# Stick-breaking attention on one core: masks ahead of logits, ScalarE in written order, weight casts three units ahead

## The chip, the cores and the metric

The kernel runs on one core of one Trainium2 chip. The metric is the device time of one execution in microseconds (us); the time of the kernel before is the median of three runs. The profile shows one execution of the same program, taken by the hardware profiler. Engines are called as the profile calls them: PE (TensorE, matmuls), DVE (VectorE), ACT (ScalarE), POOL (GpSimd), SP (SyncE, which issues most DMAs).

## The reference

A trunk of four layers on 256 frames of width 1024 in float32: layers 0 and 3 mix tokens by retention, layer 1 by a Conformer convolution, layer 2 by stick-breaking attention; each is followed by a squared-ReLU MLP. The change touches layer 2 alone:

```
def stick_breaking_mixer(xn, w_in, q_gain, k_gain, w_out):
    proj = xn @ w_in
    q, k, v = jnp.split(proj, 3, axis=-1)
    q = rms_norm(q by head, q_gain); k = rms_norm(k by head, k_gain)     # 16 heads of 64
    ...
    z = einsum('bhqd,bhkd->bhqk', q, k) * scale                           # blocks of 128 queries
    mask = s_idx[None, :] < t_idx[:, None]
    log_1mb = where(mask, log_sigmoid(-z), 0.0)
    log_w = log_sigmoid(z) + cumsum(log_1mb, reverse=True) - log_1mb
    a = where(mask, exp(log_w), 0.0)
    ...
    return (a @ v, heads joined) @ w_out
```

## The kernel before

Nearly all the time is matmuls with streamed weights. A *unit* is a tile of 128x1024 float32 weights. For each unit, SP brings it by DMA (two units to one transfer of 1 MB, into one of three `raw` tiles), ACT casts it to a rounded high part `wh` (`nc.scalar.copy`, L350), DVE subtracts to get the low part `wl` (L357), and PE multiplies with both. `wh` and `wl` have five buffers each. The function `unit` does this; the order of the units is fixed by the list `PLAN`.

In `stick`, the string `SB_ORDER` gives the order of steps, each a letter and its indices: `p b kb` is one weight unit of the projection of q and k for head group b (four heads; `mm_a`, 12 matmuls of 512 columns, L918 to L920); `n b` is the RMS norm of that group (two Squares on ACT, L1372; on DVE two sums L1374, a chain of small operations for the inverse root, and two scalings L1384); `u b` and `t b` transpose q and k on PE (L1394) and copy them out on ACT (L1399, L1406); `l b` makes the logits of the group in three PSUM tiles: z2 (second 128 queries against second 128 keys, L1420) and z0, z1 (first 128 keys against all queries, for the even and the odd heads, L1433); the mask is added by a matmul of an identity with a tile of 0 and -1e30 (L1427). `s b` is the softplus of the three tiles (ACT Abs L1445, Exp L1446, Ln L1447; DVE max-and-add L1448, rounding L1450, remainder L1451); `w b i` adds the reverse cumulative sum to tile i by matmuls with a triangle (L1458; L1462 for the second key block), whose operands are the rounding and the remainder, and takes the Exp on ACT (L1464); `v c kb` is a unit of the projection of v; `m b` multiplies weights and values (L1485, L1488). Logits and transposes share a PSUM pool of four tiles named `mis`: three logits tiles of one group and one more, so that a transpose needs a tile that an Exp of the group before has read. `res_pairs` with `out_proj` is the output projection.

The order of PE's instructions is as written (`manual_schedule` for PE). The other engines' instructions are put in order by the framework's scheduler, from its own estimates. On the chip each engine runs its list in order and waits at semaphores. Buffers of a pool are given out in the order of the program, and a write waits until the last reader of the buffer is done.

```
with self.tc.manual_schedule(engines={mybir.EngineType.PE}):
    go(SB_ORDER[0])
    self.out_proj("sb_w_out", j, G["y"], 2, 4, nxt, before=between)
```

Of the kernel before, what the change touches and what calls it, by code (L numbers as in the profile page):

```python
# [9 lines left out]
F32R = mybir.dt.float32r  # L10
I32 = mybir.dt.int32
AF = mybir.ActivationFunctionType
ALU = mybir.AluOpType
AX = mybir.AxisListType

P = 128
D = 1024
S = 256
# [12 lines left out]
DST = 6  # L31

SB_ORDER = (
    "p00 p01 r p02 p03 p10 n0 p11 p12 p13 u0 t0 p20 n1 l0 s0 p21 p22 w02 p23 n2 w00 u1 t1 p30 l1 p31 p32 s1"
    " w01 w12 p33 w10 u2 t2 w11 v00 n3 l2 s2 v01 v02 w22 v03 u3 t3 w20 v10 l3 v11 s3 w21 v12 w32 v13 w31 w30"
    " m0 m1",
    "m2 m3",
)

# [197 lines left out]
def v3(ap, a, b):  # L239
    return ap.rearrange("p (a b) -> p a b", a=a, b=b)  # L240


class Trunk:
# [342 lines left out]
                    nc.tensor.matmul(o[:, :S], wl[:, kk, cs], z[:, :S], start=False, stop=k == 7, **kw)  # L586
        return [self.sum_w(ps[0]), self.sum_w(ps[1])]

    def res_pairs(self, name, l, acts, nkb, group, evac, before=None):
        for g in range(4 // group):  # L590
            ps = [self.acc() for _ in range(group)]
            for kb in range(nkb):
                if before is not None:
                    before(kb)
                for p in range(group):
                    w = self.unit((name, l, "b", kb, (g * group + p) * 256))
                    self.mm_b(ps[p], w, acts, kb * 4, kb == 0, kb == nkb - 1)
                    if kb == nkb - 1:
                        evac(g * group + p, ps[p])


    def ffn(self, i, nxt):
        nc = self.nc
        last = nxt is None
# [113 lines left out]
    def retention(self, j, nxt):  # L718
# [107 lines left out]
        for h in range(RH):  # L826
# [21 lines left out]
            rs = self.rsqrt(m, 2, "v")  # L848
            G = self.col(2, "G")
            nc.vector.tensor_mul(G, rs, fh)  # L850
            gn = [self.bigt() for _ in range(2)]
# [8 lines left out]
            for t in range(2):  # L860
                sg, u = self.bigt(), self.tmp()
                nc.scalar.activation(out=sg, in_=pg[t], func=AF.Silu, scale=self.r[:, t : t + 1])
                nc.vector.scalar_tensor_tensor(
                    out=u, in0=yb[t], scalar=G[:, t : t + 1], in1=gn[0], op0=ALU.mult, op1=ALU.mult
                )
# [19 lines left out]
    def out_begin(self, nxt, bias=None):  # L885
# [15 lines left out]
            self.norm_pair(p, *nxt)  # L901

        return evac

    def out_proj(self, name, l, y, nkb, group, nxt, bias=None, before=None):
        self.res_pairs(name, l, lambda k: y[k], nkb, group, self.out_begin(nxt, bias), before)


    def mm_a(self, ps, w, kb):
        nc = self.nc  # L910
# [430 lines left out]
    def stick(self, j, nxt):  # L1341
        nc = self.nc
        self.table("natural_log_exp_and_others")
        kw = dict(skip_group_check=True)
        Ur, m1r, idr, negr = (self.cp.tile([P, P], F32R, name=f"{k}r", tag=f"{k}r") for k in ("U", "m1", "id", "neg"))
        for t, key in ((Ur, "U"), (m1r, "m1"), (idr, "id"), (negr, "neg")):
            nc.vector.tensor_copy(t, self.c(key, P))
        G = {}


        def proj(b, kb):
            if kb == 0:
                G["p", b] = self.acc(), self.acc()
            w = self.unit(("sb_w_in", j, "qk", kb, b * 256))
            self.mm_a(G["p", b], w, kb)

        def rnorm():
            self.norm_r(False)

            G["r64"], G["rr"] = self.col(2, "r64"), self.col(4, "rr")  # L1360
            nc.vector.tensor_scalar(out=G["r64"], in0=self.r2, scalar1=1.0 / DH, scalar2=None, op0=ALU.mult)
# [27 lines left out]
        def trans(b, isk=1):  # L1389

            pt = self.mis()
            for pr in range(2):
                for t in range(2):
                    nc.tensor.transpose(  # L1394
                        pt[:, pr * S + t * P : pr * S + (t + 1) * P],
                        G["sc", b, t][:, isk * S + pr * P : isk * S + (pr + 1) * P], self.id,
                    )
            G["qk"[isk], b] = self.bigt()
            nc.scalar.activation(out=G["qk"[isk], b], in_=pt, func=AF.Copy, scale=self.p(("sq", "sk")[isk]))  # L1399
            if not isk:  # L1400

                G["f", b] = f = self.bigt()
                nc.gpsimd.memset(f, 0.0)
                for e in range(2):
                    r = slice(e * DH, (e + 1) * DH)
                    nc.scalar.activation(  # L1406
                        out=v3(f[r, e * S : (e + 1) * S], 2, P), in_=v3(pt, 2, S)[r, :, P:], func=AF.Copy,
                        scale=self.p("sq")[r],
                    )

        def logits(b):


            z2, z0, z1 = self.mis(), self.mis(), self.mis()
            zb = G["z", b] = [z0, z1, z2]
            kT, qT = G["k", b], G["q", b]
            for e in range(2):
                for pr in range(2):
                    o = (2 * e + pr) * P
                    nc.tensor.matmul(  # L1420
                        zb[2][:, o : o + P], kT[:, pr * S + P : (pr + 1) * S], G["f", b][:, o : o + P],
                        start=o == 0, stop=False, **kw,
                    )

            def mask(z):
                n = z.shape[1]
                nc.tensor.matmul(z, idr, negr.unsqueeze(1).to_broadcast([P, n, P]), start=False, stop=True, **kw)  # L1427

            mask(v3(zb[2], 4, P))
            for pr in range(2):  # L1430
                for e in range(2):
                    r = slice(e * DH, (e + 1) * DH)
                    nc.tensor.matmul(  # L1433
                        zb[e][:, pr * S : (pr + 1) * S], kT[r, pr * S : pr * S + P], qT[r, pr * S : (pr + 1) * S],
                        start=pr == 0, stop=False, **kw,
                    )
            for e in range(2):
                mask(v3(zb[e], 2, S)[:, :, :P])

        def soft(b):  # L1440

            zb = G["z", b]
            for i in (2, 0, 1):
                ab, ex, ln, l = self.tmp(), self.tmp(), self.tmp(), self.tmp()
                nc.scalar.activation(out=ab, in_=zb[i], func=AF.Abs)  # L1445
                nc.scalar.activation(out=ex, in_=ab, func=AF.Exp, scale=-1.0)  # L1446
                nc.scalar.activation(out=ln, in_=ex, func=AF.Ln, bias=1.0)  # L1447
                nc.vector.scalar_tensor_tensor(out=l, in0=zb[i], scalar=0.0, in1=ln, op0=ALU.max, op1=ALU.add)  # L1448
                lh, ll = self.bigt(F32R), self.bigt(F32R)
                nc.vector.tensor_copy(lh, l)  # L1450
                nc.vector.tensor_sub(ll, l, lh)  # L1451
                G["l", b, i] = lh, ll

        def weights(b, i):

# [10 lines left out]
        def values(cb, kb):  # L1466
            if kb == 0:
                G["pv", cb] = self.acc(), self.acc()
            pv = G["pv", cb]
            w = self.unit(("sb_w_in", j, "a", kb, 2 * D + cb * 512))  # L1470
            self.mm_a(pv, w, kb)
            if kb == 3:
                for t in range(2):
                    G["v", cb, t] = self.bigt()
                    nc.scalar.activation(out=G["v", cb, t], in_=pv[t], func=AF.Copy, scale=self.r[:, t : t + 1])

        def mix(b):
            A = [G["A", b, i] for i in range(3)]
# [13 lines left out]

        G["y"] = []
        table = {
            "p": proj, "r": rnorm, "n": norm, "u": lambda b: trans(b, 0), "t": trans, "l": logits, "s": soft, "w": weights, "v": values, "m": mix
        }
        def go(steps):
            for step in steps.split():
                table[step[0]](*(int(c) for c in step[1:]))

        def between(kb):
            if kb == 1:
                go(SB_ORDER[1])

        with self.tc.manual_schedule(engines={mybir.EngineType.PE}):
            go(SB_ORDER[0])
            self.out_proj("sb_w_out", j, G["y"], 2, 4, nxt, before=between)

    def run(self):
        self.table("silu_and_others")  # L1510
# [49 lines left out]
```

## Time and profile before

| | |
|---|---|
| time, median of 3 runs (lowest to highest) | 1342.24 us (1342.0 to 1342.4) |
| span of the profiled execution, first to last instruction | 1340.3 us |
| PE busy | 1330.8 us, 99% of the span |
| DVE, ACT, POOL busy | 984.0, 781.3, 134.0 us |
| granted TensorE clock, mean | 0.999 |
| layer 2's attention, from the first projection matmul to the first of the value product | 661.4 to 750.5 us of the span |

The profiled execution is given by its span alone; the median of the timed runs lies 1.9 us above it. A busy PE is read with care: matmuls overlap, and the profile models their ends, so a row's length (0.39 us for 512 columns) is longer than the distance from one start to the next (0.23 us). Where a row of the timeline has "x8", the time is that of eight matmuls together; a float32 matmul shows as two.

### The profile page before, as it was taken

What the parts mean: (1) busy time and instruction counts of PE and PEld (TensorE: products, weight loads), DVE (VectorE), ACT (ScalarE), POOL (GpSimd) and SP (SyncE); (2) the same over time, 40 slices, a digit from 0 to 9 for tenths busy, and PEclk for the clock granted to TensorE, in tenths of its full rate; (3) what the DMA queues carried; (4) which work ended last, traced back from release to release, by engine and by line L of the source; (5) the groups of instructions that cost most, each with busy time, mean ns of one, the idle gap of its engine ahead of it and who ended that gap; (6) DMA issues with size and microseconds to landing.
All of it is one profiled execution on the core that took longest, in us unless ns stands there. A gap on an engine that the chain in (4) does not pass through costs nothing.

```text
span 1340.3 us, 20902 instructions
## 1 busy us (share of the span) xinstructions
PE 1330.8 (99%) x8285; PEld 1170.4 (87%) x8285; DVE 984.0 (73%) x1642; ACT 781.3 (58%) x1205; POOL 134.0 (10%) x123
## 2 busy tenths in 40 slices
PE   9999999999999999999999999999999999999998
PEld 7988888888999998888878898888888888988886
DVE  6977769775688698765687587755697777788643
ACT  7555546664457477744578577744565555555442
POOL 3200002000169210000100010000120000100000
PEclk9999999999999999999999999999999999999999
DMA  7555555555545645555453345555555454555551
GB/s 283 210 184 190 187 181 197 189 188 189 188 159 145 219 170 203 190 192 192 172 183 126 126 166 190 192 190 194 177 181 187 174 188 173 189 189 189 204 188 63
DMA packets 41586, 244.56 MB, mean 182 GB/s; under 512 B 4624, under 2 KB 9104, under 8 KB 14096
## 3 DMA queue, kind: packets, MB, share of 16 engines
q1 hardware_dynamic: 40768, 240.86, 50.7%
q10 hardware_dynamic: 720, 2.36, 0.5%
q8 instruction: 65, 1.06, 0.3%
q14 instruction: 33, 0.27, 0.1%
HBM read 241.27 MB, written 1.93 MB: 181 GB/s over the span
## 4 chain that ended last, share of the span: by engine, by line
PE 99%; DMA 0%; ACT 0%; DVE 0%; issue 0%; SPq 0%
PE acc L524 34%; PE acc L520 18%; PE acc L683 6%; PE acc L918 6%; PE acc L920 6%; PE acc L919 6%; PE acc L504 4%; PE acc L505 4%; PE acc L506 4%; PE acc L1087 1%; PE acc L1220 1%; PE mis L809 1%; PE mis L870 1%; PE mis L400 0%; PE mis L1458 0%; PE acc L585 0%
## 5 line engine op out<-in xcount | busy, mean ns | idle before, releaser
L357 DVE TENSOR_TENSOR wl<-raw,wh 128x1024 fp32r<-128x1024 f32 (+1 forms) x440 | 546.5, 1247 | 242.8 <-ACT wh L350 236.4
L350 ACT CAST wh<-raw 128x1024 fp32r<-128x1024 f32 (+1 forms) x440 | 456.5, 1042 | 353.1 <-PE acc L524 164.8
L524 PE MATMUL acc<-z,wh 128*128 128x512 f32 x1120 | 387.4, 392 | 0.0
L520 PE MATMUL acc<-z,wl 128*128 128x256 f32 x1120 | 310.2, 281 | 0.0
L524 PE MATMUL acc<-big,wh 128*128 128x512 f32 x864 | 298.8, 392 | 0.0
L524 PEld LDWEIGHTS acc<-z,wh 128*128 128x128 f32 x1120 | 208.3, 187 | 44.7
L520 PE MATMUL acc<-big,wl 128*128 128x256 f32 x864 | 238.5, 280 | 0.5 <-DVE t L568 0.5
L520 PEld LDWEIGHTS acc<-z,wl 128*128 128x128 f32 x1120 | 211.1, 189 | 1.7
L524 PEld LDWEIGHTS acc<-big,wh 128*128 128x128 f32 x864 | 161.0, 187 | 34.8
L520 PEld LDWEIGHTS acc<-big,wl 128*128 128x128 f32 x864 | 162.4, 189 | 2.3 <-DVE t L568 1.3
L918 PE MATMUL acc<-wh,z 128*128 128x512 f32 x352 | 138.0, 392 | 0.0
L920 PE MATMUL acc<-wh,z 128*128 128x512 f32 x352 | 137.3, 390 | 0.0
L919 PE MATMUL acc<-wl,z 128*128 128x512 f32 x352 | 137.2, 390 | 0.0
L455 POOL TENSOR_TENSOR t<-t,t 128x512 f32<-128x512 f32 x23 | 36.2, 1573 | 893.7 <-ACT t L450 850.6
L567 ACT COPY t<-acc 128x256 f32<-128x256 f32 x176 | 61.8, 373 | 100.6 <-PE acc L524 99.3
L568 DVE TENSOR_TENSOR t<-acc,t 128x256 f32<-128x256 f32 x176 | 69.1, 421 | 34.9 <-ACT t L567 34.8
L683 PE MATMUL acc<-wh,big 128*128 128x512 f32 x256 | 79.3, 390 | 0.0
L920 PEld LDWEIGHTS acc<-wh,z 128*128 128x128 f32 x352 | 66.1, 188 | 14.7 <-issue 0.8
L918 PEld LDWEIGHTS acc<-wh,z 128*128 128x128 f32 x352 | 66.1, 188 | 14.1 <-issue 0.8
L919 PEld LDWEIGHTS acc<-wl,z 128*128 128x128 f32 x352 | 66.1, 188 | 13.1
L504 PE MATMUL acc<-z,wh 128*128 128x256 f32 x256 | 72.5, 284 | 0.0
L505 PE MATMUL acc<-z,wh 128*128 128x256 f32 x256 | 72.4, 283 | 0.0
(259 smaller groups left out, 1813.0 us busy)
## 6 DMA issues: line engine op xcount, KB each, us to landing
raw<-in_w SPq DMA_DIRECT2D x214, 1024.0 KB, 4.8
raw<-in_w SPq DMA_DIRECT2D x8, 512.0 KB, 8.9
big<-in_gn SPq DMA_DIRECT2D x16, 256.0 KB, 5.2
raw<-hd SPq DMA_DIRECT2D x8, 263.0 KB, 4.8
raw<-hd SPq DMA_DIRECT2D x8, 131.5 KB, 3.6
x<-in_x SPq DMA_DIRECT2D x4, 256.0 KB, 6.3
wh<-in_w ACTq DMA_DIRECT2D x2, 512.0 KB, 6.4
wl<-in_w ACTq DMA_DIRECT2D x2, 512.0 KB, 8.5
```

Of the source, the lines that this page charges most:

```text
L350: nc.scalar.copy(hi[:, s], src[:, s])
L357: self.nc.vector.tensor_sub(lo[:, s], src[:, s], hi[:, s])
L504: nc.tensor.matmul(o, wh[:, kk, cs], ah, start=st, stop=False, **kw)
L505: nc.tensor.matmul(o, wh[:, kk, cs], al, start=False, stop=False, **kw)
L520: mm = nc.tensor.matmul(ps[m][:, :S], wl[:, kk, cs], a[:, :S], start=first and kk == 0, stop=False, **kw)
L524: nc.tensor.matmul(ps[m], wh[:, kk, cs], a, start=False, stop=last and kk == 3, **kw)
L567: nc.scalar.copy(o[:, s], ps[m][:, S:])
L568: nc.vector.tensor_add(o[:, s], ps[m][:, :S], o[:, s])
L683: self.tc.keep_in_program_order(nc.tensor.matmul(ps[t], l, r[:, kk], start=False, stop=kb * 2 + kk == 31 and n == 2, **kw))
L918: nc.tensor.matmul(ps[t], zh[:, s], wh[:, kk], start=k == 0, stop=False, skip_group_check=True)
L919: nc.tensor.matmul(ps[t], zh[:, s], wl[:, kk], start=False, stop=False, skip_group_check=True)
L920: nc.tensor.matmul(ps[t], zl[:, s], wh[:, kk], start=False, stop=k == 7, skip_group_check=True)
```

## The change

Four things change, all in `stick`; the arithmetic stays, up to the order in which the sums of a logits tile are formed.

1. In `logits`, the mask matmuls come first and start the accumulation; before, the mask of each tile came after its logits.
2. ACT joins PE in the written order (`manual_schedule`), so that the scheduler no longer places ACT's instructions in the attention layer and its output projection. For this the softplus is split into one step per tile (`s b i`) and placed between projection units, the copy of v out of PSUM is a step of its own (`c`), and the norms move: `n1` and `n3` to ahead of the projection unit that they stood behind (`p20`, `v00`), `n2` to behind the transposes that it stood ahead of.
3. `weight(n)` calls `unit` for units up to n + 3 (`SB_AHEAD`) when unit n is used, so that ACT's casts stand three units ahead in the written order; before, the scheduler placed them.
4. `res_pairs` and `out_proj` are written out in `stick`, with the same order of matmuls.

```
 SB_ORDER = (
-    "p00 p01 r p02 p03 p10 n0 p11 p12 p13 u0 t0 p20 n1 l0 s0 p21 p22 w02 p23 n2 w00 u1 t1 p30 l1 p31 p32 s1"
-    " w01 w12 p33 w10 u2 t2 w11 v00 n3 l2 s2 v01 v02 w22 v03 u3 t3 w20 v10 l3 v11 s3 w21 v12 w32 v13 w31 w30"
-    " m0 m1",
+    "p00 p01 r p02 p03 p10 n0 p11 p12 p13 u0 t0 n1 p20 l0 s02 p21 s00 p22 s01 w02 p23 w00 u1 t1 n2 p30 l1 s12 p31 s10"
+    " p32 s11 w01 w12 p33 w10 u2 t2 w11 n3 v00 l2 s22 v01 s20 v02 s21 w22 v03 u3 t3 w20 c0 v10 l3 s32 v11 s30 w21 v12 s31"
+    " w32 v13 w31 w30 c1 m0 m1",
     "m2 m3",
 )
+SB_AHEAD = 3
...
+        keys = [("sb_w_in", j, "qk", kb, b * 256) for b in range(4) for kb in range(4)]
+        keys += [("sb_w_in", j, "a", kb, 2 * D + c * 512) for c in range(2) for kb in range(4)]
+        keys += [("sb_w_out", j, "b", kb, p * 256) for kb in range(2) for p in range(4)]
+        ready = {}
+
+        def weight(n):
+            while len(ready) <= min(n + SB_AHEAD, len(keys) - 1):
+                ready[len(ready)] = self.unit(keys[len(ready)])
+            return ready[n]
...
             zb = G["z", b] = [z0, z1, z2]
             kT, qT = G["k", b], G["q", b]
+
+            def mask(z):
+                n = z.shape[1]
+                nc.tensor.matmul(z, idr, negr.unsqueeze(1).to_broadcast([P, n, P]), start=True, stop=False, **kw)
+
+            mask(v3(z2, 4, P))
+            for e in range(2):
+                mask(v3(zb[e], 2, S)[:, :, :P])
...
-            mask(v3(zb[2], 4, P))
...
-            for e in range(2):
-                mask(v3(zb[e], 2, S)[:, :, :P])
...
-        def soft(b):
...
+        def soft(b, i):
...
-        with self.tc.manual_schedule(engines={mybir.EngineType.PE}):
+        with self.tc.manual_schedule(engines={mybir.EngineType.PE, mybir.EngineType.Activation}):
             go(SB_ORDER[0])
-            self.out_proj("sb_w_out", j, G["y"], 2, 4, nxt, before=between)
+            evac = self.out_begin(nxt)
+            ps = [self.acc() for _ in range(4)]
+            for kb in range(2):
+                if kb == 1:
+                    go(SB_ORDER[1])
+                for p in range(4):
+                    self.mm_b(ps[p], weight(24 + 4 * kb + p), lambda k: G["y"][k], kb * 4, kb == 0, kb == 1)
+                    if kb == 1:
+                        evac(p, ps[p])
```

What it moves in the built program, at three places. Names are those of the tiles with their numbers (`mis` the PSUM tiles, `big` and `t2` SBUF tiles, `wh`, `wl`, `raw` the weights), written to the left of the arrow. The line numbers of the changed kernel lie some lines off those of the profile before.

PE, the logits of the first head group, before:

```order
L1420 MATMUL mis_1321_7413<-big_1303_7355,big_1305_7364 128x128 x4
L1427 MATMUL mis_1321_7413<-negr_7150,idr_7149 128x512
L1433 MATMUL mis_1322_7414<-big_1302_7353,big_1305_7364 128x256
L1433 MATMUL mis_1323_7415<-big_1302_7353,big_1305_7364 128x256
L1433 MATMUL mis_1322_7414<-big_1302_7353,big_1305_7364 128x256
L1433 MATMUL mis_1323_7415<-big_1302_7353,big_1305_7364 128x256
L1427 MATMUL mis_1322_7414<-negr_7150,idr_7149 128x2x128
L1427 MATMUL mis_1323_7415<-negr_7150,idr_7149 128x2x128
```

and now:

```order
L1411 MATMUL mis_1328_7427<-negr_7150,idr_7149 128x512
L1411 MATMUL mis_1329_7428<-negr_7150,idr_7149 128x2x128
L1411 MATMUL mis_1330_7429<-negr_7150,idr_7149 128x2x128
L1419 MATMUL mis_1328_7427<-big_1311_7371,big_1313_7380 128x128 x4
L1426 MATMUL mis_1329_7428<-big_1310_7369,big_1313_7380 128x256
L1426 MATMUL mis_1330_7429<-big_1310_7369,big_1313_7380 128x256
L1426 MATMUL mis_1329_7428<-big_1310_7369,big_1313_7380 128x256
L1426 MATMUL mis_1330_7429<-big_1310_7369,big_1313_7380 128x256
```

The three masks moved to the front; the eight matmuls are the same.

ACT, from the Ln of the first group's last tile to the copies of the second group's transposes, before:

```order
L1447 ACTIVATE t2_1338_7453<-t2_1337_7452 128x512
L1372 ACTIVATE t2_1351_7518<-acc_1306_7366 128x512
L1372 ACTIVATE t2_1353_7523<-acc_1307_7367 128x512
L350 CAST wh_1411_7732<-raw_1410_7730 128x1024
L1464 ACTIVATE big_1347_7499<-mis_1321_7413 128x512
L1464 ACTIVATE big_1360_7548<-mis_1322_7414 128x512
L1399 ACTIVATE big_1362_7555<-mis_1361_7550,prm_91 128x512
L1406 ACTIVATE big_1363_7557<-mis_1361_7550,prm_91 64x256 x2
L1399 ACTIVATE big_1365_7566<-mis_1364_7561,prm_91 128x512
```

and now:

```order
L1436 ACTIVATE t2_1350_7501<-t2_1349_7500 128x512
L1453 ACTIVATE big_1354_7513<-mis_1328_7427 128x512
L351 CAST wh_1356_7517<-raw_1355_7515 128x1024
L1453 ACTIVATE big_1358_7537<-mis_1329_7428 128x512
L1390 ACTIVATE big_1360_7544<-mis_1359_7539,prm_91 128x512
L1397 ACTIVATE big_1361_7546<-mis_1359_7539,prm_91 64x256 x2
L1390 ACTIVATE big_1363_7555<-mis_1362_7550,prm_91 128x512
L1363 ACTIVATE t2_1365_7558<-acc_1324_7409 128x512
L1363 ACTIVATE t2_1367_7563<-acc_1325_7410 128x512
```

The two Squares of norm 2 went from ahead of the first Exp to behind the copies, and the cast from ahead of the first Exp to behind it.

DVE, the second group's scalings and the first group's z2 and z0 tiles, before:

```order
L1384 TENSOR_TENSOR t2_1319_7409<-acc_1279_7251,sbf_1318_7407 128x512
L1384 TENSOR_TENSOR t2_1320_7411<-acc_1280_7252,sbf_1318_7407 128x512
L1448 SCALAR_TENSOR_TENSOR t2_1327_7430<-mis_1321_7413,t2_1326_7429 128x512
L1450 CAST big_1328_7435<-t2_1327_7430 128x512
L1451 TENSOR_TENSOR big_1329_7436<-t2_1327_7430,big_1328_7435 128x512
L357 TENSOR_TENSOR wl_1378_7621<-raw_1376_7618,wh_1377_7620 128x1024
L1448 SCALAR_TENSOR_TENSOR t2_1333_7442<-mis_1322_7414,t2_1332_7441 128x512
```

and now:

```order
L1375 TENSOR_TENSOR t2_1322_7405<-acc_1287_7267,sbf_1321_7403 128x512
L1375 TENSOR_TENSOR t2_1323_7407<-acc_1288_7268,sbf_1321_7403 128x512
L1437 SCALAR_TENSOR_TENSOR t2_1334_7444<-mis_1328_7427,t2_1333_7443 128x512
L1439 CAST big_1335_7449<-t2_1334_7444 128x512
L358 TENSOR_TENSOR wl_1339_7456<-raw_1337_7453,wh_1338_7455 128x1024
L1440 TENSOR_TENSOR big_1336_7450<-t2_1334_7444,big_1335_7449 128x512
L1437 SCALAR_TENSOR_TENSOR t2_1343_7474<-mis_1329_7428,t2_1342_7473 128x512
```

A weight subtraction now stands between the rounding and the remainder of a logits tile. Over the twelve logits tiles this is so at seven; before, at two.

More of the change, by code (lines that the diff above doesn't have):

```diff
@@ L587, in pairs_qk @@
         return [self.sum_w(ps[0]), self.sum_w(ps[1])]
[L589 to L599, printed above, removed]
     def ffn(self, i, nxt):
@@ L903, in out_begin @@
         return evac
-    def out_proj(self, name, l, y, nkb, group, nxt, bias=None, before=None):
-        self.res_pairs(name, l, lambda k: y[k], nkb, group, self.out_begin(nxt, bias), before)
     def mm_a(self, ps, w, kb):
@@ L1353, in proj @@
                 G["p", b] = self.acc(), self.acc()
-            w = self.unit(("sb_w_in", j, "qk", kb, b * 256))
-            self.mm_a(G["p", b], w, kb)
+            self.mm_a(G["p", b], weight(4 * b + kb), kb)
         def rnorm():
@@ L1421, in logits @@
                         zb[2][:, o : o + P], kT[:, pr * S + P : (pr + 1) * S], G["f", b][:, o : o + P],
-                        start=o == 0, stop=False, **kw,
+                        start=False, stop=False, **kw,
                     )
-            def mask(z):
-                n = z.shape[1]
-                nc.tensor.matmul(z, idr, negr.unsqueeze(1).to_broadcast([P, n, P]), start=False, stop=True, **kw)
-            mask(v3(zb[2], 4, P))
             for pr in range(2):
@@ L1434, in logits @@
                         zb[e][:, pr * S : (pr + 1) * S], kT[r, pr * S : pr * S + P], qT[r, pr * S : (pr + 1) * S],
-                        start=pr == 0, stop=False, **kw,
+                        start=False, stop=False, **kw,
                     )
-            for e in range(2):
-                mask(v3(zb[e], 2, S)[:, :, :P])
-        def soft(b):
[L1442 to L1452, printed above, removed]
+        def soft(b, i):
+            z = G["z", b][i]
+            ab, ex, ln, l = self.tmp(), self.tmp(), self.tmp(), self.tmp()
+            nc.scalar.activation(out=ab, in_=z, func=AF.Abs)
+            nc.scalar.activation(out=ex, in_=ab, func=AF.Exp, scale=-1.0)
+            nc.scalar.activation(out=ln, in_=ex, func=AF.Ln, bias=1.0)
+            nc.vector.scalar_tensor_tensor(out=l, in0=z, scalar=0.0, in1=ln, op0=ALU.max, op1=ALU.add)
+            lh, ll = self.bigt(F32R), self.bigt(F32R)
+            nc.vector.tensor_copy(lh, l)
+            nc.vector.tensor_sub(ll, l, lh)
+            G["l", b, i] = lh, ll
         def weights(b, i):
@@ L1469, in values, with values_out @@
             pv = G["pv", cb]
[L1470 to L1475, printed above, removed]
+            self.mm_a(pv, weight(16 + 4 * cb + kb), kb)
+        def values_out(cb):
+            for t in range(2):
+                G["v", cb, t] = self.bigt()
+                nc.scalar.activation(
+                    out=G["v", cb, t], in_=G["pv", cb][t], func=AF.Copy, scale=self.r[:, t : t + 1]
+                )
         def mix(b):
@@ L1494, in stick @@
         table = {
-            "p": proj, "r": rnorm, "n": norm, "u": lambda b: trans(b, 0), "t": trans, "l": logits, "s": soft, "w": weights, "v": values, "m": mix
+            "p": proj, "r": rnorm, "n": norm, "u": lambda b: trans(b, 0), "t": trans, "l": logits, "s": soft, "w": weights, "v": values, "c": values_out, "m": mix
         }
@@ L1499, in go @@
                 table[step[0]](*(int(c) for c in step[1:]))
-        def between(kb):
-            if kb == 1:
-                go(SB_ORDER[1])
-        with self.tc.manual_schedule(engines={mybir.EngineType.PE}):
+        with self.tc.manual_schedule(engines={mybir.EngineType.PE, mybir.EngineType.Activation}):
             go(SB_ORDER[0])
-            self.out_proj("sb_w_out", j, G["y"], 2, 4, nxt, before=between)
+            evac = self.out_begin(nxt)
[7 more added lines that the diff above has]
+                        evac(p, ps[p])
     def run(self):
```

## The prediction

> **What bounds the kernel now.** I read the page first, for the share of each engine and the clock, then the waits of PE, since only what PE loses can be won.
>
> ```profile
> span 1340.3 us, 20902 instructions
> PE 1330.8 (99%) x8285; PEld 1170.4 (87%) x8285; DVE 984.0 (73%) x1642; ACT 781.3 (58%) x1205; POOL 134.0 (10%) x123
> PEclk9999999999999999999999999999999999999999
> ...
> PE mis L292 <- POOL t L270: 1.3, 1, 1.3
> PE mis L1394 <- ACT big L1464: 1.0, 1, 1.0
> PE acc L585 <- ACT wh L350: 0.6, 1, 0.6
> PE acc L520 <- DVE t L568: 0.5, 2, 0.2
> ```
>
> PE is busy 99% of the span at full clock. Of its listed waits only one lies in the attention layer: 1.0 us before a transpose (L1394), ended by an Exp on ACT (L1464). L292, L585 and L520 are at the start and in other layers and are not touched. So PE is the bound in this stage, and a change to ACT's order is worth at most the wait that ACT causes. The timeline of PE shows the wait, that of ACT its cause:
>
> ```profile
> 698.93 0.62 PE L1458 MATMUL mis<-big,Ur 128*128 128x512 f32 x2
> 699.38 0.40 PE L1462 MATMUL mis<-big,m1r 128*128 128x256 f32 x2
> 699.62 0.60 PE L1394 MATMUL mis<-cst,t 128*128 128x128 f32 x4
> 701.21 0.66 PE L1394 MATMUL mis<-cst,t 128*128 128x128 f32 x4 [0.99 <-ACT big L1464]
> ...
> 698.45 1.28 ACT L1372 ACTIVATE t<-acc 128x512 f32<-128x512 f32 x2 [0.91 <-PE acc L920]
> 699.62 1.04 ACT L350 CAST wh<-raw 128x1024 fp32r<-128x1024 f32 x1
> 700.56 1.09 ACT L1464 ACTIVATE big<-mis 128x512 f32<-128x512 f32 x2
> 701.52 0.70 ACT L1399 ACTIVATE big<-mis,prm 128x512 f32<-128x512 f32 x1
> 702.09 0.95 ACT L1406 ACTIVATE big<-mis,prm 64x256 f32<-64x256 f32 x2
> 703.07 0.69 ACT L1399 ACTIVATE big<-mis,prm 128x512 f32<-128x512 f32 x1
> ```
>
> The second transpose of group 1 needs a PSUM tile which the first Exp of group 0 reads. That Exp starts at 700.56 because two Squares of norm 2 (1.28) and a weight cast (1.04) stand ahead of it on ACT; the transpose follows 0.65 us later.
>
> **The change part by part.** *ACT's order.* Now the Exp of z2 stands directly behind the last Ln, with Squares and cast behind it. PE reaches w02, whose result the Exp reads, one projection unit (12 matmuls, priced below) ahead of w00 and the transposes, so the Exp has some 2.7 us for its 0.6. The wait goes: -1.0 us. What is late next is norm 2, now behind the copies: its Squares follow the last copy (0.6 us after 703.07) instead of starting at 698.45, some 5 us later; its consumer u2 is behind the four units p30 to p33 and the logits, over 10 us of PE, so it stays covered, and so does the release of its PSUM tiles, next needed by v00.
>
> *Masks first.* The logits group and the plain projection around it:
>
> ```profile
> 684.05 1.03 PE L1394 MATMUL mis<-cst,t 128*128 128x128 f32 x8
> 684.84 0.47 PE L918 MATMUL acc<-wh,z 128*128 128x512 f32 x1
> 685.15 0.39 PE L919 MATMUL acc<-wl,z 128*128 128x512 f32 x1
> 685.38 0.39 PE L920 MATMUL acc<-wh,z 128*128 128x512 f32 x1
> ...
> 687.67 1.05 PE L1420 MATMUL mis<-big,big 128*128 128x128 f32 x8
> 688.48 0.48 PE L1427 MATMUL mis<-negr,idr 128*128 128x512 f32 x1
> 688.89 1.13 PE L1433 MATMUL mis<-big,big 64*128 64x256 f32 x8
> 689.95 0.50 PE L1427 MATMUL mis<-negr,idr 128*128 128x256 f32 x2
> 690.29 0.39 PE L918 MATMUL acc<-wh,z 128*128 128x512 f32 x1
> 690.52 0.39 PE L919 MATMUL acc<-wl,z 128*128 128x512 f32 x1
> ```
>
> From start to start, a 512-column matmul takes 0.23 (690.29 to 690.52), so a unit of 12 takes 2.72 to 2.76. The group takes 0.81 + 0.41 + 1.06 + 0.34 = 2.62 us. The 512-column mask takes 0.41 where 0.23 is plain, and the two of 256 columns 0.34 where the L1462 pair above takes 0.24: 0.28 us beyond the plain price, at the places where PE passes from 128x128 float32 matmuls to a mask, to half-height ones (64x128) and back. The row at 684.84 shows one such loss alone: the first projection matmul after transposes takes 0.31, 0.08 more than its followers. Now the masks follow a projection matmul of the same kind, which saves one such passage in each group (L1420 to mask); the passages into and out of the half-height matmuls remain, the last one paid by the next projection matmul. Lower end of the gain: 0 (the loss moves along whole); upper end 0.28. I take 0.09, the size of the loss shown alone: four groups, -0.4 us, between 0 and -1.1. The Trainium skill, "TensorEngine Tiling (Array Packing)", section "Tiling Modes", says that changing the tiling mode drains the TensorE. Their number is two a group before and after, so by that rule alone this part saves nothing and the sum would be 0.4 us higher; the row at 684.84 shows a loss with no change of mode, which is why I keep the 0.09.
>
> *Softplus by tiles, and what DVE does in between.* The matmuls of w02 need the remainder of z2 from DVE. Group 0 is the tightest, since norm 1's chain now stands ahead of it on DVE:
>
> ```profile
> 684.20 1.37 DVE L1374 TENSOR_REDUCE sbs<-t 128x8 f32<-128x512 f32 x2 [0.37 <-ACT t L1372]
> 685.48 0.35 DVE L1375 TENSOR_SCALAR qkm<-sbs,r 128x8 f32<-128x8 f32 x2
> 685.82 1.23 DVE L357 TENSOR_TENSOR wl<-raw,wh 128x1024 fp32r<-128x1024 f32 x1
> 686.96 0.17 DVE L384 TENSOR_SCALAR qky<-qkm 128x16 int32<-128x16 int32 x1
> 688.41 0.17 DVE L395 SCALAR_TENSOR_TENSOR qky<-qkt,qky 128x16 f32<-128x16 f32 x1
> 690.09 0.17 DVE L1381 TENSOR_TENSOR sbf<-qky,rr 128x16 f32<-128x16 f32 x1
> 690.29 1.29 DVE L1384 TENSOR_TENSOR t<-acc,sbf 128x512 f32<-128x512 f32 x2
> 691.50 0.68 DVE L1448 SCALAR_TENSOR_TENSOR t<-mis,t 128x512 f32<-128x512 f32 x1
> 692.21 0.43 DVE L1450 CAST big<-t 128x512 fp32r<-128x512 f32 x1
> 692.67 0.69 DVE L1451 TENSOR_TENSOR big<-t,big 128x512 fp32r<-128x512 f32 x1
> ...
> 689.00 0.60 ACT L1445 ACTIVATE t<-mis 128x512 f32<-128x512 f32 x1
> 690.29 0.63 ACT L1447 ACTIVATE t<-t 128x512 f32<-128x512 f32 x1
> ```
>
> Let T be the start of the group's first mask. PE asks for the remainder at the second matmul of w02: 2.5 (the group) + 5.5 (p21, p22) + 0.2 = T + 8.2. DVE's list up to it, by these rows: sums and scalars 1.6, a weight subtraction 1.1 (685.82 to 686.96), the root's chain 1.6, the factor 0.2, scalings 1.2, max-and-add 0.7, rounding 0.5, the inserted subtraction 1.1, remainder 0.7: 8.7 to 8.8. It starts with norm 1's first Square, which ACT does behind the copies of the transposes: these become ready about 2.9 before T (p20's 2.7 and half of the 0.8 of the transposes, less the end of the last one, 0.2), take 2.15 (701.52 to 703.07, and 0.6), the Square 0.6, so T - 0.1 to T - 0.3. The softplus on ACT, 1.9 from Abs to the end of Ln, begins when z2's logits are done, before T + 2, and is not what DVE waits for. The remainder is there at T + 8.4 to T + 8.7: PE waits 0.2 to 0.5 there by these sums, and 0 if the steps follow each other a few hundredths closer. Groups 1 and 2 have the same list with a transpose stage more on PE, and group 3 has no norm. I take +0.3 in all (0 to +0.9).
>
> *Casts three ahead.* The cover of each weight is three units of PE, 8.2 us, against a cast and a subtraction of 1.04 + 1.23 and the work that stands ahead of them. SP's queue: a raw tile comes free with the subtraction of its second unit, some five us ahead of PE's use of it (8.2 less 2.3 and a softplus step), and the next cast from it is due two units and more later; the transfer takes 4.8:
>
> ```profile
> raw<-in_w SPq DMA_DIRECT2D x214, 1024.0 KB, 4.8
> ```
>
> So no transfer becomes late; cost 0. Without this cover a late unit would cost PE up to the 2.3 of cast and subtraction. POOL's memsets keep their place ahead of the f tiles; the written-out projection and the copy of v keep PE's order: 0.
>
> Sum: -1.0 - 0.4 + 0.3 = -1.1 us on a span of 1340.3, so 1339.2; the median of the timed runs lies 1.9 above the span, and I carry that over: 1342.24 - 1.1 = 1341.1 us. A change of 0.2% is 2.7 us, about what a measurement of this kernel can tell from none.
>
> **The rivals.** *The wait only moves.* The waits at w02 come to the upper end, 0.9 or a little more, and the masks save nothing: -1.0 + 0.9 = -0.1, 1342.1 us. For it: the margin on DVE is negative by my own sums. Against: only three tiles are tight.
>
> *DVE's split starves PE (slower).* At seven of the twelve tiles a weight subtraction now stands between rounding and remainder. If PE paid its 1.14 in full at each, that is +8.0, with the gains 1348.8 us. It counts as slower only when these seven cost over 4.1 us together, about 0.6 each. Against: behind each group's first tile the next ones have a projection unit of PE apart, and the DVE is 73% busy.
>
> *More was hidden in the busy PE (faster).* In the logits group 0.28 us of 2.62 is lost inside busy time. With all of it won in four groups and no new wait: -1.0 - 1.1 = -2.1, 1340.1 us. To pass 2.7 something outside these groups must gain. For it: PE's 99% need not be PE at its best, the loads of weights being 87% in the page's row. The Trainium skill, "Trainium Kernel Development and Optimization", section "Performance Expectations", says this as a rule: matmul busy time is a bad metric because matmuls are pipelined, and that of the loads a good one. Against: in the projection units, most of the stage, matmuls already start every 0.23 us.
>
> *Nothing changes:* ACT's order in the build is different at the very place of the wait, so this is not a case of its own; it falls into the first rival.
>
> **How the numbers follow.** My sum, 1340.5 to 1341.7 us: 0.60. The wait only moves, 1341.7 to 1343.5: 0.20. More won, below 1340.5: 0.14, of it below 1339.5: 0.06. Slower by over 2.7 us: 0.05 (0.01 between). The range 1340.0 to 1342.9 reaches at its low end to the whole of the faster rival's -2.1, at its high end 0.8 above the first rival's time (another 0.3 at each of the three tight tiles), and leaves out about 2 in 10. Faster 0.06, same 0.89, slower 0.05.
>
> **What would show it.** Right: the list of PE's waits has no L1394; the logits groups take 2.4 to 2.6 us from first mask to the next projection matmul; small waits, if any, before the triangle matmuls (L1447 of the changed kernel) of groups 0 and 2, ended by DVE. ACT's rows show Exp ahead of the cast. Wrong: waits of a projection matmul for a cast or a subtraction (cover gone), or waits before most of the triangle matmuls, or a span that moves though the stage from 661 to 750 us keeps its length.

## The result: 1345.7 us, slower by 0.2%, and lost outside the changed stage

The changed kernel takes 1345.70 us (median of 12 runs, 1344.49 to 1346.42) against 1342.47 (12 runs, 1341.77 to 1343.71): a ratio of 1.0022 [1.0014, 1.0030]. The forecast was 1341.1, in a range of 1340.0 to 1342.9. The profiled execution has a span of 1344.2 against 1340.3.

The page and the list of PE's waits, after (the last five rows: what waited for what, us in total, times, longest):

```profile
span 1344.2 us, 20909 instructions
PE 1333.9 (99%) x8285; PEld 1169.4 (87%) x8285; DVE 983.0 (73%) x1642; ACT 779.4 (58%) x1205; POOL 135.7 (10%) x123
...
PE mis L293 <- POOL t L271: 1.3, 1, 1.3
PE acc L1071 <- issue: 1.2, 1, 1.2
PE acc L507 <- DVE wl L358: 0.7, 1, 0.7
PE acc L586 <- ACT wh L351: 0.5, 1, 0.5
PE acc L521 <- DVE t L569: 0.5, 2, 0.2
```

The 1.0 us wait of the transposes is gone, as forecast, and no listed wait in the attention layer has come in its place. PE has the same number of matmuls but is busy 3.1 us longer: what was lost is inside busy time, where no list of waits shows it. To find the stage, take the starts of three matmuls: the first of layer 2's attention projection, the first of its output projection, and the first of layer 3's projections behind layer 2's MLP. PE's timeline, before:

```profile
661.36 0.40 PE L918 MATMUL acc<-wh,z 128*128 128x512 f32 x1
...
753.31 0.38 PE L504 MATMUL acc<-big,wh 128*128 128x256 f32 x1
...
951.95 0.28 PE L504 MATMUL mis<-big,wh 128*128 128x256 f32 x1
```

and after:

```profile
662.63 0.40 PE L902 MATMUL acc<-wh,z 128*128 128x512 f32 x1
...
753.61 0.38 PE L505 MATMUL acc<-big,wh 128*128 128x256 f32 x1
...
955.32 0.28 PE L505 MATMUL mis<-big,wh 128*128 128x256 f32 x1
```

Attention took 91.95 us and now takes 90.98: -0.97, near the -1.1 of the forecast. The output projection with layer 2's MLP took 198.64 and now takes 201.71: +3.07, in a stage whose code is not in the diff. What lies behind it went from 388.35 to 388.88 (+0.53), what lies ahead from 661.36 to 662.63 (+1.27). The last is no effect of the change: of the kernels further down, new_order_in_before, which up to there has the program of the kernel before, starts attention at 662.16, and order_only, with the change, at 660.70. 1.2 us of it is the listed wait at L1071, in layer 1; order_only, with the same code there, has none. The other three differences add up to +2.6, and the ratio's interval, 1.9 to 4.0 us, holds that.

Layer 2's MLP is one stream in which `mm_w` alternates matmuls of 256 columns (wl) and of 512 (wh). PE's groups between 810 and 930 us, deep inside it, with their count, busy time and mean ns of one; before:

```profile
L524 PE MATMUL acc<-big,wh 128*128 128x512 f32 x177 | 61.4, 391 | 0.0
L524 PE MATMUL acc<-z,wh 128*128 128x512 f32 x170 | 59.0, 391 | 0.0
L520 PE MATMUL acc<-big,wl 128*128 128x256 f32 x177 | 49.6, 280 | 0.0
L520 PE MATMUL acc<-z,wl 128*128 128x256 f32 x170 | 47.6, 280 | 0.0
```

and after:

```profile
L525 PE MATMUL acc<-z,wh 128*128 128x512 f32 x172 | 60.8, 399 | 0.0
L525 PE MATMUL acc<-big,wh 128*128 128x512 f32 x169 | 59.8, 399 | 0.0
L521 PE MATMUL acc<-z,wl 128*128 128x256 f32 x172 | 48.3, 281 | 0.0
L521 PE MATMUL acc<-big,wl 128*128 128x256 f32 x169 | 47.5, 281 | 0.0
```

In the same 120 us 347 pairs ran before and 341 after, with no idle time in either; the 512-column matmul has gone from 391 to 399 ns. The single rows show how. Before:

```profile
819.64 0.39 PE L524 MATMUL acc<-z,wh 128*128 128x512 f32 x1
819.87 0.28 PE L520 MATMUL acc<-z,wl 128*128 128x256 f32 x1
819.99 0.39 PE L524 MATMUL acc<-z,wh 128*128 128x512 f32 x1
...
820.68 0.39 PE L524 MATMUL acc<-z,wh 128*128 128x512 f32 x1
```

and after:

```profile
819.76 0.40 PE L525 MATMUL acc<-z,wh 128*128 128x512 f32 x1
820.00 0.28 PE L521 MATMUL acc<-z,wl 128*128 128x256 f32 x1
820.11 0.40 PE L525 MATMUL acc<-z,wh 128*128 128x512 f32 x1
...
820.82 0.40 PE L525 MATMUL acc<-z,wh 128*128 128x512 f32 x1
```

Three pairs took 1.04 us and now take 1.06. In the unrounded starts the short rhythm repeats every pair, 230 + 117 ns, 346.7 a pair; the long one every third pair, 241 + 120, 236 + 113, 233 + 117, a mean of 353.3. Each lasts unchanged to the end of the stage: some 470 pairs by 6.6 ns are the 3.1 us. PE's clock is granted in full in both (PEclk 1.00). Nor is the rhythm drawn anew at each execution: the fastest of the 12 runs of the changed kernel (1344.49) is slower than the slowest of the 12 before (1343.71).

The two kernels part at one place, the row sum for the MLP's norm, a plain float32 matmul between pairs 1 and 2. Before and after:

```profile
790.66 0.59 PE L480 MATMUL mis<-t,cst 128*128 128x256 f32 x2
790.94 0.59 PE L481 MATMUL mis<-t,cst 128*128 128x256 f32 x2
```

In the pairs just ahead of it both are short by the unrounded starts: 346.7 ns a pair before, and 346.5 after, there as 112 + 233 and 117 + 231 in turn. Behind it the one goes on at 346.7 and the other is long from the second pair on.

And the order of PE ahead of it is not the same. That PE's order is as written, as was said of the kernel before, holds inside `stick` and not here. In pairs 0 to 3 of an MLP `mm_w` keeps only part of the order (`keep=p >= 4`), so the scheduler places these matmuls, and it placed the 64 of pairs 0 and 1 in another order once ACT's order was fixed. Apart from the masks, PE's order in the two built programs differs nowhere else. Rows 4430 to 4437 of PE, before:

```
L520 MATMUL acc_8392<-z_8304,wl_8397 128x256
L524 MATMUL acc_8392<-z_8304,wh_8396 128x512
L520 MATMUL acc_8393<-z_8304,wl_8397 128x256
L524 MATMUL acc_8393<-z_8304,wh_8396 128x512
L520 MATMUL acc_8392<-z_8342,wl_8417 128x256
L520 MATMUL acc_8393<-z_8342,wl_8417 128x256
L520 MATMUL acc_8451<-z_8264,wl_8456 128x256
L524 MATMUL acc_8451<-z_8264,wh_8455 128x512
```

and after:

```
L521 MATMUL acc_8451<-z_8281,wl_8456 128x256
L525 MATMUL acc_8451<-z_8281,wh_8455 128x512
L521 MATMUL acc_8451<-z_8311,wl_8456 128x256
L525 MATMUL acc_8392<-z_8311,wh_8396 128x512
L525 MATMUL acc_8393<-z_8311,wh_8396 128x512
L521 MATMUL acc_8392<-z_8314,wl_8397 128x256
L521 MATMUL acc_8393<-z_8314,wl_8397 128x256
L525 MATMUL acc_8451<-z_8311,wh_8455 128x512
```

### The profile page after: what moved, and what is told of

Its sections match the earlier page's. It is cut to its first block, busy times and chain, and to the rows that moved or that the text cites. A ratio compares the mean times of both kernels' runs of the same rounds, so it can differ in the third digit from the quotient of the medians.

```text
span 1344.2 us, 20909 instructions
## 1 busy us (share of the span) xinstructions
PE 1333.9 (99%) x8285; PEld 1169.4 (87%) x8285; DVE 983.0 (73%) x1642; ACT 779.4 (58%) x1205; POOL 135.7 (10%) x123
## 3 DMA queue, kind: packets, MB, share of 16 engines
q8 instruction: 65, 1.06, 0.3%
## 4 chain that ended last, share of the span: by engine, by line
PE 98%; DMA 1%; DVE 0%; ACT 0%; issue 0%; SPq 0%
PE acc L525 34%; PE acc L521 18%; PE acc L671 6%; PE acc L902 6%; PE acc L904 6%; PE acc L903 6%; PE acc L505 4%; PE acc L507 4%; PE acc L506 4%; PE acc L1071 1%; PE acc L1204 1%; DMA raw<-in_w 1%; PE mis L797 1%; PE mis L858 1%; PE mis L401 0%; PE mis L1447 0%
## 5 line engine op out<-in xcount | busy, mean ns | idle before, releaser
L521 PE MATMUL acc<-z,wl 128*128 128x256 f32 x1120 | 310.1, 281 | 0.0
L507 PE MATMUL acc<-z,wl 128*128 128x256 f32 x256 | 72.3, 283 | 0.7 <-DVE wl L358 0.7
L505 PE MATMUL acc<-z,wh 128*128 128x256 f32 x256 | 72.5, 284 | 0.0
```

What stands on the lines that cost most here:

```text
L505: nc.tensor.matmul(o, wh[:, kk, cs], ah, start=st, stop=False, **kw)
L507: nc.tensor.matmul(o, wl[:, kk, cs], ah, start=False, stop=en, **kw)
L521: mm = nc.tensor.matmul(ps[m][:, :S], wl[:, kk, cs], a[:, :S], start=first and kk == 0, stop=False, **kw)
```

## The experiments

Theory R: the order ahead, or any interruption, decides into which of the two rhythms the stream of layer 2's MLP falls. Rival C: the weights' casts, which ACT now does three units ahead, disturb PE there. All kernels with their results; stage lengths are differences of the three starts named above, "rest" runs from there to the last matmul:

| kernel | median us | ratio to before | attention | layer 2's MLP | rest | ns a pair |
|---|---|---|---|---|---|---|
| before | 1342.1 to 1342.6 | 1 | 91.96 | 198.64 | 381.92 | 346.7 |
| changed | 1345.70 | 1.0022 [1.0014, 1.0030] | 90.98 | 201.71 | 382.40 | 353.3 |
| masks_only | 1342.26 | 1.0001 [0.9992, 1.0009] | 91.90 | 198.64 | 381.84 | 346.7 |
| order_only | 1344.92 | 1.0020 [1.0011, 1.0029] | 91.00 | 201.71 | 382.40 | 353.3 |
| nudge_before | 1345.73 | 1.0024 [1.0015, 1.0033] | 91.96 | 201.94 | 381.74 | 353.3 |
| nudge_after | 1344.73 | 1.0017 [1.0008, 1.0025] | 91.01 | 201.74 | 382.10 | 346.7, then 353.3 |
| old_order_in_after | 1341.88 | 0.9997 [0.9988, 1.0005] | 90.96 | 198.64 | 382.33 | 346.7 |
| new_order_in_before | 1342.96 | 1.0005 [0.9996, 1.0013] | 91.96 | 198.62 | 382.35 | 346.7 |
| written_order_control | 1344.96 | 1.0019 [1.0010, 1.0028] | 91.00 | 201.71 | 382.39 | 353.3 |
| regular_nudge_in_after | 1341.77 | 0.9995 [0.9986, 1.0004] | 91.00 | 198.86 | 382.38 | 346.7 |
| late_nudge_in_after | 1345.40 | 1.0025 [1.0015, 1.0035] | 90.99 | 201.93 | 382.35 | 353.3 |
| late_nudge_in_before | 1342.83 | 1.0003 [0.9994, 1.0012] | 91.96 | 198.86 | 382.08 | 346.7 |
| late_pause_in_after | 1348.60 | 1.0045 [1.0032, 1.0058] | 91.00 | 203.87 | 382.45 | 353.3 |
| late_wide_nudge_in_after | 1343.18 | 1.0004 [0.9995, 1.0013] | 90.98 | 199.38 | 382.50 | 353.3, then 346.7 |

**The two halves of the change.** masks_only is the kernel before with the masks ahead of the logits; order_only is the changed kernel with the masks behind them, as before:

```
             zb = G["z", b] = [z0, z1, z2]
             kT, qT = G["k", b], G["q", b]
+            mask(v3(z2, 4, P))                    # masks_only; order_only has the reverse
+            for e in range(2):
+                mask(v3(zb[e], 2, S)[:, :, :P])
...
-            mask(v3(zb[2], 4, P))
...
-            for e in range(2):
-                mask(v3(zb[e], 2, S)[:, :, :P])
```

> The kernel before with the masks ahead of the logits and nothing else. Both theories: the logits groups take 2.53 instead of 2.62 us, so the attention gains 0.4 us, and the wait of 1.0 us at the transpose stays. R: the time is 1342.1 us, or 3.1 more if the MLP's stream falls into the slow pace. C: 1342.1 us, pace 346.7.

> The changed kernel with each mask behind its logits as before: the written order on ScalarE and the casts three units ahead alone. Both: the wait of 1.0 us at the transpose is gone, small waits of up to 0.3 us before the triangle matmuls. R: 1341.5 us, or 1344.6 if the MLP's stream falls into the slow pace. C: slow pace, 1345.6 us or more, since the casts lie as in the changed kernel.

The masks alone are worth next to nothing: attention 91.90 against 91.96, where 0.4 was expected. The written order of ACT with the casts three ahead has everything, the gain in attention (91.00) and the loss in the MLP (201.71), and with it PE's new order of the 64 matmuls; with masks_only PE's order there is that of before. No run separates the written order from the casts. The first logits group in PE's timeline of masks_only shows where the saving of the masks went:

```profile
687.64 0.62 PE L1419 MATMUL mis<-negr,idr 128*128 128x512 f32 x3
688.10 1.06 PE L1427 MATMUL mis<-big,big 128*128 128x128 f32 x8
689.09 1.13 PE L1434 MATMUL mis<-big,big 64*128 64x256 f32 x8
690.15 0.50 PE L918 MATMUL acc<-wh,z 128*128 128x512 f32 x1
690.49 0.39 PE L919 MATMUL acc<-wl,z 128*128 128x512 f32 x1
```

The group is shorter, 2.51 us (687.64 to 690.15) for 2.62, but the projection matmul behind the half-height ones now needs 0.34 for 0.23. The 0.18 that the first mask lost behind the 128x128 matmuls (0.41 for 0.23) is now lost by these behind the masks (0.99 for 0.81). From the last projection matmul ahead of a group to the second behind it, all four groups have 3.075 us in either order.

**A nudge.** One more 128x64 matmul right behind the row-sum matmul of layer 2's MLP, its result not used, in each kernel:

```
-    def norm_rb(self):
+    def norm_rb(self, extra=0):
...
+        if extra:
+            nc.tensor.matmul(ps[:, S : S + extra], self.c("m1", P), sq[:, :extra], start=True, stop=True, skip_group_check=True)
...
-                rb.append(... else self.norm_rb())
+                rb.append(... else self.norm_rb(64 if i == 2 else 0))
```

> The kernel before with the same small matmul at the same place. R: the pace of layer 2's MLP is 346.7 or 353.3 ns a pair, and the time 1342.6 or 1345.7 us according to it. C: the pace stays 346.7 and the time 1342.6 us, since no cast has moved.

> The changed kernel with one more small matmul (64 columns, its result is not used) behind the row-sum matmul in the third unit pair of layer 2's MLP; nothing else moves. Theory R (rhythm): a stream of alternating 256- and 512-column matmuls has two stable paces on PE, 346.7 and 353.3 ns a pair, and keeps the one into which it falls after an interruption; the changed kernel fell into the slow one over some 470 pairs of layer 2's MLP, which is 3.1 us. The small matmul gives the stream another start: either it falls into the fast pace and the time is 1342.6 us (3 below the changed kernel), or it stays slow and the time is that of the changed kernel plus 0.1. Rival C (the cause lies in the moved casts and subtractions, which now disturb PE throughout): the pace stays 353 ns, 1345.8 us.

In the kernel before, two passes of 0.14 us (790.91 to 791.05 in the timeline; 0.2 with what the next matmul loses) bring the long rhythm, 399 ns instead of 391, and 3.3 us:

```profile
790.48 0.59 PE L480 MATMUL mis<-t,cst 128*128 128x256 f32 x2
790.91 0.33 PE L482 MATMUL mis<-t,cst 128*128 128x64 f32 x2
791.05 0.37 PE L522 MATMUL acc<-z,wl 128*128 128x256 f32 x1
...
L526 PE MATMUL acc<-z,wh 128*128 128x512 f32 x172 | 60.8, 399 | 0.0
```

No cast has moved there, so rival C is not needed for the loss. In the changed kernel the same nudge brought the short rhythm for 8 us, from 791 to 799; then, in pairs 2 and 3 whose order is free too, two matmuls of 256 columns followed each other at 798.90 and two of 512 at 801.21, and behind the latter the long one was back.

**The order itself.** old_order_in_after writes the 64 matmuls of pairs 0 and 1 out in the order of the kernel before, new_order_in_before is the mirror image, and written_order_control has the same code in the changed kernel with the changed kernel's own order. All three keep pairs 2 and 3 as written:

```
+FIRST = "000l 000h 001l 001h 010l ..."     # pair, contraction step, half, wl or wh
+    def pairs_01(self, i, act):
+        for p, k, m, t in FIRST.split():
+            ...
+            self.tc.keep_in_program_order(nc.tensor.matmul(o, wt[:, k % 4, cs], x, ...))
...
-        for p in range(16):
+        if i == 2:
+            self.pairs_01(i, act)
+        for p in range(2 if i == 2 else 0, 16):
...
-    keep=p >= (2 if last else 4)
+    keep=p >= (2 if last or i == 2 else 4)
```

> The changed kernel, with the 64 matmuls of layer 2's MLP pairs 0 and 1 written out in the order in which TensorE has them in the kernel before (pairs 2 and 3 kept in the order of writing); ScalarE's written order, masks and casts stay as changed. Theory R (the pace of the alternating stream in layer 2's MLP depends on the order of the matmuls ahead of it): the stream runs at 346.7 ns a pair, the stage from the output projection to layer 3's first matmuls is 198.6 us instead of 201.7, and attention's gain of 1.0 stays: 1341.5 to 1342.0 us, a ratio of 0.9995. Rival C (the casts that ScalarE does three units ahead disturb TensorE's stream): the order changes nothing, 353.3 ns a pair and 1344.7 to 1345.7 us.

> The changed kernel with pairs 0 and 1 of layer 2's MLP written out in the order that TensorE has there already, and pairs 2 and 3 kept in the order of writing: the form of the kernel with the old order, without its order. Theory R: the order decides, so the stream falls into 353.3 ns a pair as in the changed kernel: 1344.5 to 1345.5 us. Rival F (the form helps: the regular pairs 2 and 3, or ScalarE and VectorE rows that moved with it): 346.7 ns and 1341.5 to 1342.2 us, and then the kernel with the old order has shown nothing about the order.

> The mirror image: the kernel before, with pairs 0 and 1 of layer 2's MLP in the order that TensorE has in the changed kernel; nothing else of the change. Theory R: 353.3 ns a pair, the stage 201.7 us, attention as before: 1345.3 to 1345.8 us, a ratio of 1.0023. Rival C: the casts are where they were, so 346.7 ns a pair and 1342.4 us. If the order ahead sets the pace only together with the moment at which the stream begins (a draw), either value can come, and both kernels of this pair need not exchange.

PE's groups between 810 and 930 us, old_order_in_after:

```profile
L533 PE MATMUL acc<-z,wh 128*128 128x512 f32 x169 | 58.6, 391 | 0.0
L529 PE MATMUL acc<-big,wl 128*128 128x256 f32 x178 | 49.8, 280 | 0.0
```

and written_order_control:

```profile
L533 PE MATMUL acc<-z,wh 128*128 128x512 f32 x170 | 60.1, 399 | 0.0
L529 PE MATMUL acc<-big,wl 128*128 128x256 f32 x171 | 48.0, 281 | 0.0
```

The two kernels differ in the order of PE's 64 matmuls and in the places of some rows of ACT and VectorE that go with them up to about 800 us, a few casts of the MLP among them; masks, attention and the casts three ahead are those of the change in both. One has 346.7 ns a pair and 1341.88 us, the other 353.3 and 1344.96. So the order, with the rows that go with it, makes the 3.1 us in the changed kernel. Rival C falls, and those rows do not hold the long rhythm either: late_wide_nudge_in_after, below, has every row of ACT and VectorE in the order of the changed kernel and runs at 346.7 behind its nudge. But the mirror image did not flip: with the new order the kernel before kept 346.7. The order decides only together with something else that the stream brings along, and as a rule "this order is slow" would be wrong.

**Interruptions.** regular_nudge_in_after is nudge_after with pairs 2 and 3 kept as written. The three late ones put a matmul into the regular stream ahead of pair 5: of 64 columns, of 256, or of 64 columns of a copy that VectorE makes of pair 4's sum, so that PE has to wait:

```
                 at = p == 2
+                if i == 2 and p == 5:
+                    ps = self.mis()
+                    self.tc.keep_in_program_order(nc.tensor.matmul(
+                        ps[:, :64], self.c("m1", P), self.sq[:, :64], start=True, stop=True   # or 256; or g[:, :64]
+                    ))
```

> The changed kernel with the 128x64 matmul behind the row-sum matmul of layer 2's MLP (as in the nudge run, where the stream ran at 346.7 until two matmuls of the same width followed each other 8 us later), and pairs 2 and 3 kept in the order of writing, so that nothing irregular follows. Theory R: the fast rhythm that the nudge gave then lasts to the end of the stage: 198.7 us, and 1341.6 to 1342.1 us in all. If the slow rhythm came of something that lasts (the casts, the weights' transfers), the stage falls back to 353.3 within some 10 us: 1344.7 us.

> The changed kernel with one more 128x64 matmul (its result is not used) in layer 2's MLP ahead of pair 5, where the stream has been in its slow rhythm for some 9 us and the order behind is regular to the stage's end. Theory R (the rhythm is a state of the stream that an interruption draws anew): it either stays at 353.3 (1344.8 us) or runs at 346.7 from there on, for some 380 pairs of 6.6 ns, 2.5 us less: 1342.4 us; in the trace the spacings right behind the extra matmul decide it. If the rhythm follows from the order or the operands, not from a state, the pairs behind it stay at 353.3 and only 0.1 us is added.

> The kernel before with one more 128x64 matmul ahead of pair 5 of layer 2's MLP, in the middle of the fast rhythm. If each interruption draws the rhythm anew, either outcome can come: 346.7 and 1342.3 us, or 353.3 from there on for some 380 pairs, 2.5 us more: 1344.8 us. If the rhythm behind an interruption is the one ahead of it (as the late nudge in the changed kernel showed for the slow one), it stays at 346.7: 1342.3 us.

> The changed kernel, with a real pause in the slow stream: the same 128x64 matmul ahead of pair 5, but of a copy that VectorE makes of pair 4's sum, so that TensorE waits some 0.7 to 1.5 us for it. Theory R2 (what sets the rhythm is how far TensorE's side work is ahead when the stream starts, which a pause lets catch up, as behind the 0.6 us gap at 184 us): 346.7 ns a pair from there on, 2.5 us less than the changed kernel and the pause on top: 1343.2 to 1344 us. If a pause doesn't change the rhythm either: 353.3, and 1345.7 to 1346.5 us.

> The changed kernel with a 128x256 matmul of the row sum's kind (215 ns a pass by its own records in the trace) ahead of pair 5, where a 128x64 one changed nothing. If the rhythm behind an interruption only repeats the one ahead of it: 353.3 and 0.4 us more than the changed kernel, 1345.3 us. If the length of the interruption decides: 346.7 from there on, 1342.8 us.

With nothing irregular behind it, the early nudge's short rhythm lasted to the stage's end, as expected. The late nudge of 64 columns changed neither rhythm: the long one stayed long, the short one short. A pause of 1.7 us changed nothing either:

```profile
807.56 0.39 PE L525 MATMUL acc<-z,wh 128*128 128x512 f32 x1
809.63 0.44 PE L623 MATMUL mis<-t,cst 128*128 128x64 f32 x2 [1.68 <-DVE t L629]
809.88 0.36 PE L521 MATMUL acc<-z,wl 128*128 128x256 f32 x1
...
L525 PE MATMUL acc<-z,wh 128*128 128x512 f32 x176 | 62.2, 399 | 0.0
```

and the stream still has 399 ns behind it, so R2, by which a pause lets PE's side work catch up, fell. (Its 1348.60 us, from five runs, is 2.1 above the upper end of what was expected for that case: the stage is 2.16 longer than the changed kernel's, and the rest is not explained.) The 256-column matmul, of the same shape as the row sum's, turned the long rhythm into the short one within a pair:

```profile
806.95 0.59 PE L623 MATMUL mis<-t,cst 128*128 128x256 f32 x2
807.19 0.47 PE L521 MATMUL acc<-z,wl 128*128 128x256 f32 x1
...
L525 PE MATMUL acc<-z,wh 128*128 128x512 f32 x169 | 58.6, 391 | 0.0
```

So the rhythm is a state of the stream, kept until something breaks it, and not every break does. One sign goes with the outcome at all 18 breaks of these 14 profiles (the row sum in each, the late matmul in four): where the start of the first 512-column matmul behind the break and the next start are 235 to 239 ns apart, the short rhythm follows, and where they are 229 to 231 apart, the long one. That shows where the two part and not why. By what PE goes from one into the other is open: neither the length of the break (0.2 us did at one place and 1.7 did not at another) nor the order alone gives it.

## Why the prediction was wrong

*The wait of the transposes, -1.0: right.* It was even a little more: four transposes take 0.4, so the next four would have come at 700.03 and not at 701.21. After, the eight stand in one row, with the first Exp ahead of the cast:

```profile
701.09 1.04 PE L1385 MATMUL mis<-cst,t 128*128 128x128 f32 x8
...
697.31 0.63 ACT L1436 ACTIVATE t<-t 128x512 f32<-128x512 f32 x1
697.86 0.60 ACT L1453 ACTIVATE big<-mis 128x512 f32<-128x512 f32 x1
698.36 1.04 ACT L351 CAST wh<-raw 128x1024 fp32r<-128x1024 f32 x1
```

*DVE's chain ahead of the triangle matmuls, +0.3: +0.2.* Group 0, the tightest by the working, pays:

```profile
697.03 0.80 PE L1447 MATMUL mis<-big,Ur 128*128 128x512 f32 x2
...
700.41 0.61 PE L1447 MATMUL mis<-big,Ur 128*128 128x512 f32 x2
...
696.59 0.69 DVE L1440 TENSOR_TENSOR big<-t,big 128x512 fp32r<-128x512 f32 x1
```

0.80 where 0.61 is free, without a listed wait: the second of the two matmuls starts at 697.33, when DVE's remainder ends (697.28). Group 2 pays 0.03 (0.65 for 0.62), group 1 nothing. With -1.18 for the wait this gives -0.96, the stage's -0.97. That this is so near the -1.1 of the sum is in part luck: 0.2 more at the wait and 0.1 less at DVE make up for most of the 0.4 that the masks did not bring. The seven inserted subtractions cost nothing else: the slower rival's mechanism didn't come.

*The masks, -0.4: 0.* The step that failed in this term was taking the loss at 684.84 as the price of one passage that disappears. No loss does: the 0.18 of the first mask moves to the 128x128 matmuls, and 0.11 of the two other masks to the first projection matmul behind the group. So the group's 2.51 us lie in the 2.4 to 2.6 that were to show the forecast right, and nothing is gained. The rule of the Trainium skill ("TensorEngine Tiling (Array Packing)", section "Tiling Modes": changing the tiling mode drains the TensorE) that was weighed against it, with as many changes of mode as before, gives 0, and the runs agree: 3.075 us in either order.

*The casts three ahead, 0: right* as far as attention goes; no wait of PE for a weight is in its list there.

*What brought the miss:* the step that failed was making the sum over the attention layer alone: every other stage was taken at its old length without a row, a term of 0. The order of PE was compared in attention, where the change writes it, and not in layer 2's first MLP pairs, where a scheduler places matmuls with an eye to ACT. That is the +3.07, three times the gain. Among the signs that would show the forecast wrong stood a span that moves though the stage keeps its length; no rival had a mechanism for it, so 0.05 was too little for slower. The faster rival had the right place: PE's 99% need not be PE at its best. The Trainium skill, "Trainium Kernel Development and Optimization", section "Performance Expectations", calls matmul busy time a bad metric; here PE is busy without a gap in both kernels, at paces 1.9% apart, which agrees.

*Layer 3, +0.4:* its retention stage has pieces in the long rhythm in the changed kernel and its variants (rest 382.1 to 382.5), and in new_order_in_before, against 381.7 to 382.1 in the other runs of the kernel before. It looks like the same effect; no run took it apart.

## What to carry to other kernels

When a scheduler sets part of an order, fixing one engine's order moves others in stages that the diff doesn't touch: compare every engine's order over the whole program, not only around the edit. When PE is busy all the time, a stage is checked by its pace, matmuls of one form in a fixed window or their mean duration (391 or 399 ns here), since a loss of 3 us in busy time is in no list of waits. Old_order_in_after keeps the change's 1.0 us in attention and is some 3 us better than the changed kernel; against the kernel before its runs show no gain clear of noise (0.9997 [0.9988, 1.0005]).

## What the runs showed of the hardware

- A stream that alternates 256- and 512-column matmuls has two lasting rhythms, 346.7 and 353.3 ns a pair, with PE's clock granted in full in both. The Trainium skill, "TensorE: Matmul & The Clock Gate", section "Back-to-back issue gap", gives N / 2.4 + 2.5 ns for a single matmul at full clock, by which an estimate for the pair is 325 ns, and says that this is too much for a stream at 512 columns, where it has about 131 ns. Here both paces lie above the estimate, by 7 and 9%, and a 512-column matmul of the stream takes 230 to 241 ns from its start to the next; the measurement decides.
- One matmul that costs 0.2 us made a kernel 3.3 us slower (1.0024 [1.0015, 1.0033]) by changing the rhythm of what followed, and one of 256 columns some 16 us later in the other kernel turned it back.
- A real pause of 1.7 us, in late_pause_in_after, did not change the rhythm.
- Masks ahead of or behind half-height matmuls: 3.075 us both ways. The first form behind a passage paid for it in either order: 0.18 us between the 128x128 matmuls and the masks, 0.11 behind the half-height ones.
